# A hybrid encoder trunk on one core: the first attention queries moved ahead of the retention's second output projection, and the last two steps of a norm ranked as urgent

## The chip, the core and the metric

The kernel runs on one NeuronCore of a Trainium2 chip. The metric is the device time of one execution in microseconds (us); several runs are made and their median is compared. TensorE (PE) does the matmuls, VectorE (DVE) and ScalarE (ACT) the elementwise work, GpSimd (POOL) a few small operations and the accumulating DMAs, and SyncE (SP) issues all other DMAs.

## What is computed

Two layers of a hybrid mixer on a sequence of 512 tokens with 1024 channels, all in float32:

```python
def hybrid_layer(x, ...):
    h = rms_norm(x, norm_g)
    z = h @ w_in
    (c_glu, c_gate, r_q, r_k, r_v, r_gate, a_q, a_k, a_v, a_gate, g_logit) = jnp.split(z, offsets, axis=-1)
    y_conv = conv_module(c_glu, c_gate, conv_dw, conv_b, conv_ln_g, conv_ln_b) @ w_conv_out
    y_ret = retention_branch(r_q, r_k, r_v, r_gate, ret_decay, positions) @ w_ret_out
    y_attn = window_attention_branch(a_q, a_k, a_v, a_gate, q_norm_g, k_norm_g, attn_sink, positions) @ w_attn_out
    g = jax.nn.sigmoid(g_logit + b_gate).reshape(B, S, N_BRANCH, D)
    merged = g[:, :, 0] * y_conv + g[:, :, 1] * y_ret + g[:, :, 2] * y_attn
    return x + merged @ w_out
```

The convolution module is a gated depthwise convolution of 31 taps, a layer norm over the channels, SiLU and a gate. The retention has 4 heads (keys of 256, values of 512 channels) in both directions, a norm per head and a gate. The attention has 16 query heads of 64 channels and 4 key/value heads, a norm and a partial rotation of queries and keys, a window of 128 tokens to each side and a sink.

## The kernel before, in words

**Precision and tiles.** Every float32 operand of a matmul is kept as a rounded high part and a low part (the rest). One product of 128 rows is three matmuls: high by high, high by low, low by high (`mm3`). ScalarE makes the high part by a copy; VectorE makes the low part by a subtraction, or, for the weights named in `BY_DMA` (among them `or`, the retention's output projection), ScalarE writes the negated high part and a DMA that GpSimd issues adds the weight to it in SBUF. A weight tile `wraw` (128 x 1024) comes from DRAM on SP's queue into one of 4 buffers; `wh` and `wl` have 8 buffers each, of half a weight tile.

**Order.** The builder writes the program down as a list of operations, each with an engine, its dependences and a priority: the time on TensorE at which it was written down plus an offset, the urgency. `Plan.order` then plays the program through with a table of costs. On each engine it always takes, of the operations that are ready, the one with the smallest priority, and the order found so is the fixed program order of each engine; on the chip every engine takes its instructions in that order. Line 342, where the recorded instructions are issued, is therefore the line of all of them in the profile, and they are told apart by their tiles. PSUM has two pools of 4 banks, `pc` and `ps`.

**Layer.** `layer` runs four retention heads (`head`), then `attention`, then `finish`. Two tables place the rest of the work between them: `HEAD_FILL` names for each head h what is written down after its queries and values (h, 0), after its scores and values product (h, 1), after its transposes and gate products (h, 2), and, for odd h, between the columns of the output projection (h, "o"). There m counts the entries; for h = 3 they count from 1. The letters: C and T are input and taps of the convolution, R, S, L, K, P gate projections, V the keys and values of the attention (`kv`), W the transposes of the normed keys (`k_transposes`), and Q the projection of four query heads with their norm (`Q`). `ATT_FILL` does the same in attention; there X0 and X1 are the first two steps of `conv_stats`.

**The stretch around the first edit.** At the end of head 3 the program transposes the head's normed output (tile `on`, a `big` tile; 16 transposes with the identity in `cst`, 4 per bank of `ps`), VectorE multiplies each bank with its gate (`pp<-ps,pp`) and makes the low part (`big<-pp,big`), as it does for the other head, which is fetched from DRAM (`og`). These are the operands of the second output projection: 8 columns m = 0 to 7 of 24 matmuls each, weights `or`, in banks of `pc`. Before the change V0 stands at (3, 1) and its projection runs just ahead of the transposes; the norm of the keys (`qk_norm`: squares, sums `qk_v`, a power on GpSimd `qk_r`, products, all in a `ws` tile) is in VectorE's queue beside the gate products. W0 stands at (3, 2), and Q0 at (3, "o") with m = 1, so between columns 0 and 1. Q0 is 96 matmuls of 128x256 in two banks of `ps`, from two weight tiles.

**The stretch around the second edit.** `conv_stats` makes the layer norm's statistics of the convolution in four steps. Step 2 (after column 0 of the attention's output projection, `FIN_FILL`) sums the squares over the channels by four matmuls with `ones` (`pc<-ones,ws`), VectorE and GpSimd make the reciprocal root (`tr_v`, `tr_r`), and VectorE writes four diagonal blocks (`ws<-cst,tr_r`). Step 3 (after column 3) spreads them by one matmul (`pc<-ws,ones`), and ScalarE copies the result. `conv_finish` uses it.

Of the kernel before, what the change touches and what calls it, by code (L numbers as in the profile page):

```python
# [36 lines left out]
NORM_EARLY, EVAC_EARLY, SQUARES_LATE = -15000, -20000, 0  # L37
LOAD_EARLY, SPLIT_EARLY, TAPS_LATE, STATS_LATE = -20000, -16000, 150000, 15000
# [7 lines left out]

HEAD_FILL = {(0, 0): "P6 P7", (0, 1): "R0 R1 C0 T0", (0, 2): "C1 C2 R2 R3",
             (1, 0): "C3", (1, 1): "C4 C5 T1", (1, 2): "C6 R4", (1, "o"): "R5 C7 L0 L1 L2 S0 S1 S2", (2, 0): "T2 S3", (2, 1): "T3 R6", (2, 2): "T4 K0 K1 R7",
             (3, 0): "T5 K2", (3, 1): "T6 T7 K3 V0", (3, 2): "W0", (3, "o"): "Q0"}


C_A, C_B, C_GATE = 0, 1024, 2048
# [326 lines left out]
class Builder:  # L379
# [531 lines left out]
    def conv_stats(self, step):  # L911

        nc = self.nc
        y = lambda k: self.fetch("y", k, self.tile("yt", [P, S]), step == 0)
        with nc.urgency(STATS_LATE):
            if step == 0:
                cs = self.tile("ws", [P, 2, S])
                self.cs, self.rb = cs[:, 0, :], cs[:, 1, :]
                nc.vector.tensor_tensor(out=self.cs, in0=y(0), in1=y(1), op=ALU.add)
                for k in range(2, 8):  # L920
                    nc.vector.tensor_tensor(out=self.cs, in0=self.cs, in1=y(k), op=ALU.add)
            elif step == 1:
                pm = self.pc()
                self.mm(pm, self.ones, self.cs, True, True)
                for k in range(8):
                    yk = y(k)
                    nc.vector.scalar_tensor_tensor(out=yk, in0=pm, scalar=-1.0 / D, in1=yk, op0=ALU.mult, op1=ALU.add)
                    sq = self.rb if k == 0 else self.tile("pad", [P, S])
                    nc.scalar.activation(out=sq, in_=yk, func=AF.Square)
                    self.keep("yc", k, yk)  # L930
                    if k:
                        nc.vector.tensor_tensor(out=self.rb, in0=self.rb, in1=sq, op=ALU.add)
            elif step == 2:
                self.rstd_diag(self.rb, self.cs)
            else:
                nc.scalar.copy(out=self.rb, in_=self.spread(self.cs))
# [321 lines left out]
```

## Time and profile before

| what | value |
|---|---|
| median of 3 runs | 1960.28 us (1959.76 to 1960.9) |
| the profiled execution | 1959.06 us |
| its span, first to last instruction | 1957.3 us |
| mean granted TensorE clock | 0.998 |
| TensorE busy | 1931.5 us, 99% |
| VectorE busy | 1694.7 us, 87% |
| ScalarE busy | 1159.7 us, 59% |
| GpSimd busy | 230.3 us, 12% |
| moved by DMA | 348.98 MB, mean 178 GB/s |

A profile is one execution. Busy is the time in which an engine had an instruction running; matmuls are pipelined, so the time of one reaches into the next, and the distance between starts tells the pace. A wait is put down to the operation that ended last before the waiting instruction began. The granted clock is the share of TensorE's full speed that the chip allowed.

### The profile page before, as it was taken

Reading aid. Unit: us, or ns where it says so; the run is one execution under the profiler, and the core shown is the slowest. Engines: PE = TensorE matmul, PEld = TensorE weight load, DVE = VectorE, ACT = ScalarE, POOL = GpSimd, SP = SyncE. Lnnn points to the kernel's source line nnn. Section 1 sums busy time; section 2 is a strip of 40 time slices with the busy share of each in tenths; the row PEclk is TensorE's granted clock in tenths of the full one; section 3 lists DMA queues with packets and bytes.
Section 4 is the critical chain, followed back from the end, with each engine's and each line's share of the span. In section 5 each row is a group of like instructions: output and inputs, shape, how many; then the busy total and the mean of one; then the engine's idle time right before and its main releaser. Section 6 shows DMA issues by size and latency. Waiting matters only on the chain.

```text
span 1957.3 us, 32895 instructions
## 1 busy us (share of the span) xinstructions
PE 1931.5 (99%) x11812; PEld 1717.1 (88%) x11812; DVE 1694.7 (87%) x3122; ACT 1159.7 (59%) x2230; POOL 230.3 (12%) x284
## 2 busy tenths in 40 slices
PE   8999999999999999999999999999999989999999
PEld 6899999999987888878889999999899878887787
DVE  8989998899987898977688999989999788989772
ACT  5565566556555478854436555655565465789541
POOL 0001011110123010000000010111101240110000
PEclk9999999999999999999999999999999999999999
DMA  6377478765678623488523665787656785234772
GB/s 231 91 212 188 135 221 216 207 168 181 181 180 230 202 77 103 148 273 280 169 87 114 213 167 149 219 212 208 170 177 171 211 218 190 86 100 155 252 268 72
DMA packets 143875, 348.98 MB, mean 178 GB/s; under 512 B 16096, under 2 KB 16352, under 8 KB 143712
## 3 DMA queue, kind: packets, MB, share of 16 engines
q1 hardware_dynamic: 115776, 296.02, 45.2%
q0 software_dynamic: 27936, 50.87, 15.1%
q8 instruction: 92, 1.51, 0.3%
q14 instruction: 71, 0.58, 0.1%
HBM read 237.25 MB, written 58.72 MB: 151 GB/s over the span
## 4 chain that ended last, share of the span: by engine, by line
PE 91%; DVE 3%; issue 3%; DMA 2%; POOL 0%; ACT 0%; SPq 0%; POOLq 0%; DVEq 0%
PE pc L342 57%; PE ps L342 34%; DVE ws L342 1%; DMA wraw<-wpk 1%; DMA oa<-pp 1%; DVE yt L342 1%; POOL qk_r L342 0%; DVE wide L342 0%; DVE pp L342 0%; DMA pp<-cg 0%; DMA wl<-wraw 0%; DVE big L342 0%; DMA big<-xT 0%; DMA yt<-y 0%; DVE mid L342 0%
## 5 line engine op out<-in xcount | busy, mean ns | idle before, releaser
L342 PE MATMUL pc<-big,wh 128*128 128x256 f32 (+1 forms) x4848 | 1150.4, 327 | 9.9 <-DVE big L342 7.8
L342 PEld LDWEIGHTS pc<-big,wh 128*128 128x128 f32 x4848 | 809.2, 188 | 91.7 <-DVE big L342 11.0
L342 PE MATMUL pc<-big,wl 128*128 128x256 f32 (+1 forms) x2424 | 789.2, 327 | 0.0
L342 ACT CAST wh<-wraw 128x512 fp32r<-128x512 f32 x558 | 344.3, 621 | 399.6 <-PE pc L342 255.7
L342 PEld LDWEIGHTS pc<-big,wl 128*128 128x128 f32 x2424 | 455.1, 188 | 37.0 <-DVE wl L342 0.3
L342 DVE SCALAR_TENSOR_TENSOR yt<-pad,prm,yt 128x512 f32<-128x512 f32 x480 | 358.3, 746 | 4.4
L342 PE MATMUL ps<-wh,big 128*128 128x512 f32 (+1 forms) x1152 | 296.8, 346 | 6.8 <-ACT big L342 6.8
L342 DVE TENSOR_TENSOR wl<-wraw,wh 128x512 fp32r<-128x512 f32 x364 | 247.3, 685 | 33.9 <-ACT wh L342 31.1
L342 POOL DMA_DIRECT2D wl<-wraw x194 | 169.4, 900 | 851.1 <-ACT wl L342 498.8
L342 ACT CAST wh<-ws 128x512 fp32r<-128x512 f32 x264 | 162.1, 621 | 157.9 <-PE pc L342 81.2
L342 PEld LDWEIGHTS ps<-wh,big 128*128 128x128 f32 x1152 | 199.7, 189 | 36.2 <-ACT big L342 6.8
L342 PE MATMUL ps<-wl,big 128*128 128x512 f32 (+1 forms) x576 | 199.0, 346 | 0.0
L342 DVE TENSOR_TENSOR wl<-ws,wh 128x512 fp32r<-128x512 f32 x264 | 177.5, 685 | 5.4 <-ACT wh L342 4.5
L342 PE MATMUL ps<-big,wh 128*128 128x256 f32 x832 | 151.3, 279 | 0.0
L342 ACT ACTIVATE wl<-wraw 128x512 fp32r<-128x512 f32 x194 | 122.5, 632 | 15.5 <-PE ps L342 15.5
L342 PEld LDWEIGHTS ps<-big,wh 128*128 128x128 f32 x832 | 127.0, 188 | 0.2
L342 PEld LDWEIGHTS ps<-wl,big 128*128 128x128 f32 x576 | 108.8, 189 | 14.8 <-issue 0.2
L342 PE MATMUL ps<-big,wl 128*128 128x256 f32 x416 | 116.0, 279 | 0.0
L342 DVE TENSOR_TENSOR ws<-wraw 128x512 f32<-128x512 f32 x132 | 86.8, 684 | 15.0 <-DMA wraw<-wpk 14.9
L342 PE MATMUL ps<-big 128*128 128x512 f32 (+2 forms) x448 | 99.5, 345 | 0.1
L342 PEld LDWEIGHTS ps<-big 128*128 128x128 f32 x448 | 81.6, 188 | 16.9 <-DVE sm_m L342 1.0
L342 DVE TENSOR_TENSOR ws<-ws,wraw 128x512 f32<-128x512 f32 x132 | 90.2, 683 | 0.1
(124 smaller groups left out, 2092.5 us busy)
## 6 DMA issues: line engine op xcount, KB each, us to landing
wraw<-wpk SPq DMA_DIRECT2D x312, 512.0 KB, 4.1
wl<-wraw POOLq DMA_DIRECT2D x194, 256.0 KB, 5.2
g<-pp SPq DMA_DIRECT2D x48, 256.0 KB, 3.3
pp<-g SPq DMA_DIRECT2D x48, 256.0 KB, 4.3
rg<-pp SPq DMA_DIRECT2D x32, 256.0 KB, 2.7
pp<-rg SPq DMA_DIRECT2D x32, 256.0 KB, 4.6
yt<-y SPq DMA_DIRECT2D x32, 256.0 KB, 2.9
wide<-toe SPq DMA_DIRECT2D x16, 448.0 KB, 3.4
```

Of the source, the lines that this page charges most:

```text
L342: getattr(getattr(self.nc, op.engine), op.method)(**kw)
```

## The change

Two lines. In `HEAD_FILL`, Q0 moves from (3, "o") to (3, 2) and stands ahead of W0 there, so it is written down ahead of the key transposes and of all columns of the second output projection, and its two weight tiles come ahead of column 0's in the weights' order. In `conv_stats`, steps 2 and 3 get the urgency `EVAC_EARLY` (-20000) instead of `STATS_LATE` (+15000); steps 0 and 1 keep theirs.

```diff
@@ -46,7 +46,7 @@
 HEAD_FILL = {(0, 0): "P6 P7", (0, 1): "R0 R1 C0 T0", (0, 2): "C1 C2 R2 R3",
              (1, 0): "C3", (1, 1): "C4 C5 T1", (1, 2): "C6 R4", (1, "o"): "R5 C7 L0 L1 L2 S0 S1 S2", (2, 0): "T2 S3", (2, 1): "T3 R6", (2, 2): "T4 K0 K1 R7",
-             (3, 0): "T5 K2", (3, 1): "T6 T7 K3 V0", (3, 2): "W0", (3, "o"): "Q0"}
+             (3, 0): "T5 K2", (3, 1): "T6 T7 K3 V0", (3, 2): "Q0 W0"}
@@ -912,7 +912,7 @@
-        with nc.urgency(STATS_LATE):
+        with nc.urgency(STATS_LATE if step < 2 else EVAC_EARLY):
```

**First place: TensorE in layer 0, from the end of the keys' and values' projection (`ps<-wh,big` 128x512).** `ps<-cst,big` are the transposes of `on`, `pc<-big,wh` and `pc<-big,wl` the columns of the output projection, `ps<-wh,big` 128x256 is Q0, `ps<-cst,ws` are the key transposes. Before:

```order
L342 MATMUL ps<-wh,big 128x512
L342 MATMUL ps<-cst,big 128x128 x4
L342 MATMUL pc<-big,wh 128x512 x2
L342 MATMUL pc<-big,wl 128x512
L342 MATMUL ps<-cst,big 128x128 x12
L342 MATMUL pc<-big,wh 128x512 x2
L342 MATMUL pc<-big,wl 128x512
```

and with the change, first the start and then the end of Q0:

```order
L342 MATMUL ps<-wh,big 128x512
L342 MATMUL ps<-cst,big 128x128 x16
L342 MATMUL ps<-wh,big 128x256
L342 MATMUL ps<-wl,big 128x256
L342 MATMUL ps<-wh,big 128x256 x2
```

```order
L342 MATMUL ps<-wl,big 128x256
L342 MATMUL ps<-wh,big 128x256
L342 MATMUL pc<-big,wh 128x512
L342 MATMUL ps<-cst,ws 128x128 x8
L342 MATMUL pc<-big,wh 128x512
L342 MATMUL pc<-big,wl 128x512
```

All of Q0 now stands between the transposes of `on` and column 0, and the key transposes stand behind Q0 and one matmul of column 0; before, column 0 came first, then the key transposes, then Q0. In layer 1 one matmul of column 0 stays between the twelfth and the thirteenth transpose; the rest is the same.

**Second place: VectorE beside it in layer 0.** `big<-ps,big` are the low parts of the keys' and values' banks, `wl<-wraw,wh` weight splits (Q0's), `pp<-ps,pp` the gate products, `big<-pp,big` the low parts of the projection's operands, `qk_v` and `ws<-ws,qk_r` the norm of the keys. Before:

```order
L342 TENSOR_TENSOR big<-ps,big 128x4x64
L342 TENSOR_TENSOR big<-pp,big 128x512
L342 TENSOR_TENSOR big<-ps,big 128x4x64
L342 TENSOR_TENSOR wl<-wraw,wh 128x512 x2
L342 TENSOR_TENSOR pp<-ps,pp 128x512
L342 TENSOR_TENSOR big<-ps,big 128x4x64 x2
L342 TENSOR_REDUCE qk_v<-mid 128x8 x2
L342 TENSOR_TENSOR big<-pp,big 128x512
L342 TENSOR_SCALAR qk_v<-qk_v 128x16
L342 TENSOR_TENSOR big<-pp,big 128x512 x3
L342 TENSOR_TENSOR pp<-ps,pp 128x512 x3
L342 TENSOR_TENSOR ws<-ws,qk_r 128x1024
```

and with the change:

```order
L342 TENSOR_TENSOR big<-ps,big 128x4x64 x4
L342 TENSOR_TENSOR pp<-ps,pp 128x512
L342 TENSOR_REDUCE qk_v<-mid 128x8 x2
L342 TENSOR_TENSOR big<-pp,big 128x512
L342 TENSOR_SCALAR qk_v<-qk_v 128x16
L342 TENSOR_TENSOR big<-pp,big 128x512 x4
L342 TENSOR_TENSOR pp<-ps,pp 128x512 x2
L342 TENSOR_TENSOR ws<-ws,qk_r 128x1024
```

The two splits have moved ahead of these rows, the four low parts of the keys and values now come first, and one low part of the operands and one gate product have moved behind the step on `qk_v`.

**Third place: TensorE in layer 0, at the norm's last two steps.** The long rows are the columns of the attention's output projection. Before:

```order
L342 MATMUL pc<-ones,ws 128x1 x3
L342 MATMUL pc<-big,wl 128x512
L342 MATMUL pc<-big,wh 128x512 x2
L342 MATMUL pc<-big,wl 128x512
L342 MATMUL pc<-big,wh 128x512 x2
L342 MATMUL pc<-big,wl 128x512
L342 MATMUL pc<-ws,ones 128x512
```

and with the change, the steps one after the other:

```order
L342 MATMUL pc<-big,wh 128x512
L342 MATMUL pc<-ones,ws 128x1 x4
L342 MATMUL pc<-big,wh 128x512
```

```order
L342 MATMUL pc<-big,wh 128x512
L342 MATMUL pc<-ws,ones 128x512
L342 MATMUL pc<-big,wh 128x512
```

Before, one of the four matmuls with `ones` stood 48 rows ahead of the other three, and the spread 6 rows behind these. Now all four stand together, and the spread 48 rows behind them.

## Rows read from the trace of the kernel before

**Rows 1.** The page, busy us, share of the span and instructions of each engine.

```profile
PE 1931.5 (99%) x11812; PEld 1717.1 (88%) x11812; DVE 1694.7 (87%) x3122; ACT 1159.7 (59%) x2230; POOL 230.3 (12%) x284
```

**Rows 2.** TensorE's waits: line, waited for, us in total, times, longest us.

```profile
PE pc L342 <- DVE big L342: 7.8, 7, 2.6
...
PE pc L342 <- DVE ws L342: 3.1, 2, 1.6
```

**Rows 3.** TensorE's timeline, layer 0: start us, us, operation, count [idle before <-releaser].

```profile
596.75 0.60 PE L342 MATMUL ps<-cst,big 128*128 128x128 f32 x4
...
607.92 0.50 PE L342 MATMUL pc<-big,wh 128*128 128x512 f32 x1 [1.92 <-DVE big L342]
...
613.22 0.37 PE L342 MATMUL ps<-wh,big 128*128 128x256 f32 x1
...
624.20 0.39 PE L342 MATMUL pc<-big,wl 128*128 128x512 f32 x1
```

**Rows 4.** TensorE's timeline, the same stretch of layer 1.

```profile
1568.26 0.60 PE L342 MATMUL ps<-cst,big 128*128 128x128 f32 x4
...
1569.38 1.47 PE L342 MATMUL ps<-cst,big 128*128 128x128 f32 x12
...
1585.48 0.44 PE L342 MATMUL ps<-wh,big 128*128 128x256 f32 x1
```

**Rows 5.** VectorE's timeline, evacuations of two neighbouring columns of the projection, layer 0.

```profile
639.96 0.69 DVE L342 TENSOR_TENSOR pp<-pp,pc 128x512 f32<-128x512 f32 x1 [0.47 <-PE pc L342]
...
645.45 0.69 DVE L342 TENSOR_TENSOR pp<-pp,pc 128x512 f32<-128x512 f32 x1 [0.83 <-PE pc L342]
```

**Rows 6.** Windows: us, busy of PE, PEld, DVE, ACT, POOL, PEclk, DMA share, GB/s.

```profile
597.00:613.00 16.00, 11.94 (x50) 7.86 (x49) 14.45 (x28) 10.63 (x23) 7.17 (x4) 0.89 0.72 183
625.00:669.00 44.00, 44.00 (x202) 36.37 (x201) 38.83 (x67) 17.25 (x30) 10.70 (x12) 1.00 0.97 261
...
760.00:780.00 20.00, 20.00 (x142) 18.68 (x141) 15.68 (x40) 16.05 (x40) 0.38 (x2) 1.00 0.27 93
800.00:820.00 20.00, 19.89 (x99) 15.87 (x98) 19.21 (x46) 18.73 (x46) 0.47 (x2) 1.00 0.61 200
```

**Rows 7.** Timelines around the spreading matmul: TensorE and VectorE, layer 0; TensorE, layer 1.

```profile
867.88 0.40 PE L342 MATMUL pc<-big,wl 128*128 128x512 f32 x1
869.84 1.12 PE L342 MATMUL pc<-ws,ones 128*128 128x512 f32 x2 [1.56 <-DVE ws L342]
...
866.59 0.16 DVE L342 TENSOR_SCALAR tr_v<-pc 128x4 f32<-128x4 f32 x1 [0.55 <-PE pc L342]
...
868.92 0.87 DVE L342 TENSOR_SCALAR ws<-cst,tr_r 128x128 f32<-128x128 f32 x4
...
1842.33 1.12 PE L342 MATMUL pc<-ws,ones 128*128 128x512 f32 x2 [1.57 <-DVE ws L342]
```

**Rows 8.** VectorE's timeline beside the transposes and column 0, layer 0.

```profile
596.99 1.28 DVE L342 TENSOR_TENSOR wl<-wraw,wh 128x512 fp32r<-128x512 f32 x2
...
601.24 0.17 DVE L342 TENSOR_SCALAR qk_v<-qk_v 128x16 f32<-128x16 f32 x1
...
603.12 1.88 DVE L342 TENSOR_TENSOR pp<-ps,pp 128x512 f32<-128x512 f32 x3
606.03 1.23 DVE L342 TENSOR_TENSOR ws<-ws,qk_r 128x1024 f32<-128x1024 f32 x1 [1.03 <-POOL qk_r L342]
...
610.86 0.41 DVE L342 TENSOR_TENSOR ws<-mid 128x256 f32<-128x256 f32 x1
```

**Rows 9.** GpSimd's timeline, the power in the norm of the keys, layer 0.

```profile
601.49 4.51 POOL L342 TENSOR_TENSOR qk_r<-qk_v,mhalf 128x16 f32<-128x16 f32 x1 [12.63 <-DVE qk_v L342]
```

**Rows 10.** DMA issues from 600 to 665 us: operation, count, KB each, median us to landing.

```profile
wraw<-wpk SPq DMA_DIRECT2D x11, 512.0 KB, 5.3
wl<-wraw POOLq DMA_DIRECT2D x14, 256.0 KB, 5.6
...
md<-pp SPq DMA_DIRECT2D x8, 256.0 KB, 5.1
```

## The prediction, made before the changed kernel was run

> **What bounds the kernel now.** I read the page's busy shares first, then the list of who waits for whom, then TensorE's timeline in the two stretches that the change touches, and last VectorE's and the DMA there. The page says that TensorE is busy for 1931.5 of 1957.3 us [rows 1]. So nearly every microsecond that can be won is one in which TensorE stands still or runs slowly, and the list of waits says where these are [rows 2]: 7.8 us before matmuls of `pc` that wait for VectorE's `big` tiles, and 3.1 us in two places before matmuls that wait for VectorE's `ws`.
>
> The first sort sits where the second output projection of the retention begins. In layer 0 the transposes of `on` start at 596.75 us (call this T0) and the first matmul of Q0 (the queries, 128x256) starts at 613.22 [rows 3]. Between them stand 16 transposes, the 24 matmuls of column m = 0 and the 8 transposes of the normed keys. How long these take when nothing waits: 4 transposes end to end take 0.60 us and 12 take 1.47 [rows 3, 4], so 8 are 0.87 and 16 are 1.75; and a column takes 5.49 us, the distance between two evacuations of neighbouring columns (639.96 and 645.45) that both waited for TensorE [rows 5]. Together 8.11 us. The stretch took 613.22 - 596.75 = 16.47, so 8.36 us are lost, though the longest gap shown before a single matmul is 1.92 [rows 3]: each wait also empties the pipeline, and the granted clock was 0.89 in 597 to 613 us [rows 6], which is some 3.5 us at 1.2 instead of 2.4 GHz after matmuls that had come one by one, and costs half of that. Layer 1 shows the same from 1568.26 to 1585.48 [rows 4]: 17.22, so 9.11 lost. The cause is VectorE: it is busy for 14.45 of these 16 us [rows 6], with the low parts of column 0's operands, the gate products and the norm of the keys in one queue.
>
> The second sort is the spreading matmul of the convolution's norm (`pc<-ws,ones`). The matmul ahead of it starts at 867.88 and would let the next one start 0.23 later; the spread starts at 869.84 [rows 7]. That is 1.73 us, and layer 1 shows the same gap (1.57 against 1.56 [rows 7]). VectorE made the four diagonal blocks from 868.92 on, for 0.87 us [rows 7], behind a column's evacuation.
>
> **The change, part by part.** *Q0 ahead of the projection.* No matmul is added or removed. After the transposes TensorE now has Q0, 10.98 us of matmuls (613.22 to 624.20 [rows 3]) that need only weights and the old `hh`/`hl`, and column 0 comes behind it. VectorE's 14 us of work then lie beside Q0. What can still be late, per layer:
> - The transposes wait for the banks of the keys-and-values projection. Four of them and three filler matmuls of column 0 (0.44 + 0.69) filled the 1.12 us up to the next twelve in layer 1 [rows 4]. In layer 0 the fillers are gone, but the evacuations of the banks now stand first on VectorE and ScalarE. Between 0 and the fillers' 0.7; I take 0.5.
> - Q0's second bank is that of the second gate product. The last three products began at 603.12 [rows 8], so the second of all four ended about 7.0 after T0; the two weight splits (1.28 [rows 8]) no longer stand ahead of it, so 5.8. Q0 needs the bank after 1.75 + 0.5 + half of 10.98, at 7.7. Between 0 and 1; I take 0.2.
> - The key transposes now follow Q0's end, at about T0 + 13.3 (1.75 + 0.5 + 10.98). The normed keys were done at 610.86 + 0.41, T0 + 14.5 [rows 8]. Ahead of the scalar step at 601.24 that releases GpSimd's power, the two splits are gone in both layers, in layer 0 one low part of 0.6 too. The power takes 4.51 [rows 9], and what follows it from 606.03 to 611.27 is as long as before. So the keys are done 1.2 to 1.8 earlier, at 12.7 to 13.3. Bounds: 0, and 1.2 if they come no earlier than before; I take 0.5.
> - Column 0's last operand is written near the time of the keys and is wanted at its end, near T0 + 20, so that wait goes and none replaces it.
>
> This gives 8.36 + 9.11 - 2 x 1.2 = **15.1 us**. Of what the step carries along: its two weight loads (512 KB each) pass column 0's on SP's queue and are split by VectorE, so column 0's two accumulating loads are issued later on GpSimd's queue, but still ahead of the keys' power, 11 us before use. On GpSimd the second power (Q0's) now stands ahead of column 3's loads instead of column 5's. If it starts 4 us behind Q0's end (T0 + 13.3) and takes 4.51 again, they are issued near T0 + 22, land 5.6 later [rows 10], and are wanted at 13.3 + 0.87 + 3 x 5.49 = T0 + 30.6, so 3 us of cover are left; if that goes, TensorE waits what the landing takes beyond it.
>
> *The norm's last two steps as urgent.* The four matmuls with `ones` now stand together where the first of them stood, and the spread 48 rows of the order behind them, some 16 us. The diagonal is ready long before: 2 x 1.73 = 3.45 us go. In exchange 0.16 + 0.87 us of VectorE work [rows 7] stand ahead of the last operands of the attention's output projection; between 0 and 1 us per layer, I take 0.2. Net **3.0 us**. The finish of the convolution's branch starts earlier, which only adds cover.
>
> *The order inside attention* changes where the planner sees other ready times. Nothing is added. The longest single wait that the order leaves in these rows is 1.92 us [rows 3], so I bound it by -2 and +2 and take 0, since both ends are as near.
>
> Sum: 18.1 us. The profiled execution took 1959.06 us (span 1957.3 and 1.76 around it), 1.2 below the median of 1960.28. 1959.06 - 18.1 = 1941.0, and against the median 1942.2; I say 1942.
>
> **The rivals.** *Part of it comes back at once.* The key transposes stand in TensorE's queue ahead of column 0, and TensorE takes its matmuls in order: if the keys' norm is late (its power waits for squares that ScalarE does behind the evacuations) or column 3's weights are, all of it waits. For: margins of 0 to 3 us above. Against: the cover is worked out from rows. At 3 to 4 us per layer, 6 to 8 of the 18 are lost: 1948 to 1950.
>
> *VectorE takes it back in attention.* Its work is the same and has 7 us less per layer; it is busy for 19.21 of 20 us at 800 to 820 [rows 6]. If half of the time won is not absorbed, 7.5 us come back, 1950; if all of the first part, 1957. Against: it idles 4.3 of 20 us at 760 to 780 [rows 6], and its depthwise taps, which the planner ranks last, can slide towards that.
>
> *DMA becomes the bound, and the kernel slower.* A column moves 512 KB of weights, two accumulating loads of 256 KB and three tiles of 256 KB, 1.835 MB [rows 10]. While columns follow each other (625 to 669) the DMA engines are busy 0.97 of the time at 261 GB/s [rows 6]; at that pace a column would take 7.03 us, not 5.49. So far Q0 lay between columns 0 and 1 and let transfers run ahead; now eight columns follow each other. If none is covered, 16 columns x 1.54 = 24.6 us come in against 18.1: 1966.7. It decides from 6.6 us per column on (18.1 / 16 above 5.49). Against: seven columns ran at 5.49 with no gap, and much of that 0.97 is prefetch and stores that nobody waits for. The Trainium skill ("DMA: Bandwidth & Descriptors", Issuing engines are not separate DMA queues) says that transfers of SP and GpSimd share the same 16 engines, which speaks for this rival; its section Where 436 GB/s comes from puts a core's HBM limit near 358 GB/s, by which a column would need 5.1 us, the rival would fall away and the sum would stand. No stretch in the rows settles it: 261 GB/s is what was moved, not what could be.
>
> *The second part does nothing* (the matmuls with `ones` wait for the sum of squares instead): 3 us less, 1945, inside the range.
>
> **How the numbers follow.** Forecast, with the second part doing nothing inside it: 0.65, from 1938.5 (all 17.5 + 3.45 us, and a little of attention) to 1946. First rival 0.16, second 0.13 (0.03 of it within 0.2% of before), DMA 0.06 (0.02 of it with so much covered that nothing changes, 0.04 slower). Up to 1952 lie the first two and half of the second rival, 0.87, less what falls beside the forecast's bounds: 1938.5 to 1952. About 0.2%, 3.9 us, is what a measurement of this kernel can tell from no change: faster 0.91, same 0.05, slower 0.04.
>
> **What would show it.** In the new profile, the stretch from the transposes of `on` to the end of Q0 and column 0 takes 20 to 21 us instead of 27.5, with granted clock 1.00; the wait for `big` in the list falls from 7.8 to about 1; Q0's matmuls follow the transposes; the keys' transposes have at most 1 us ahead of them. The wait for `ws` before the spread is gone. The forecast is wrong if TensorE waits for `ws` or `ps` ahead of the key transposes for several us, if columns stand more than 5.6 us apart, or if gaps of more than 1 us appear in attention.

## The result and the profile after

The changed kernel took 1945.78 us (median of 4 runs, 1945.19 to 1946.74), the kernel before, on the same chip, 1960.59 (1959.76 to 1961.76). The ratio is 0.9924, with a 95% interval of 0.9909 to 0.9940: 14.8 us faster, where 18 were forecast. The profiled execution took 1945.19 us, with a span of 1943.4; before it was 1957.3, so the two traces account for 13.9 us.

The page of the changed kernel and its list of TensorE's waits, to be read against [rows 1, 2]:

```profile
PE 1927.2 (99%) x11812; PEld 1716.9 (88%) x11812; DVE 1692.2 (87%) x3122; ACT 1160.5 (60%) x2230; POOL 227.3 (12%) x284
```
```profile
PE ps L342 <- ACT big L342: 7.2, 1, 7.2
PE ps L342 <- DVE pp L342: 3.0, 5, 0.9
PE ps L342 <- DVE sm_m L342: 1.1, 3, 0.6
PE ps L342 <- ACT pp L342: 0.4, 2, 0.2
PE pc L342 <- DVE pp L342: 0.3, 1, 0.3
```

Both waits that the change aimed at are gone: 7.8 us for `big` and 3.1 for `ws`. The first line is the program's start, as it was before. What is new stands in lines two and three: 1.1 us for `sm_m`, and 3.0 for `pp`, where 1.8 were before.

TensorE's timeline of the changed kernel shows layer 0's stretch of [rows 3] and, from 1561.64 on, layer 1's of [rows 4]:

```profile
596.41 2.02 PE L342 MATMUL ps<-cst,big 128*128 128x128 f32 x16
598.37 0.39 PE L342 MATMUL ps<-wh,big 128*128 128x256 f32 x1
...
609.37 0.39 PE L342 MATMUL pc<-big,wh 128*128 128x512 f32 x1
609.60 1.03 PE L342 MATMUL ps<-cst,ws 128*128 128x128 f32 x8
...
1561.64 1.64 PE L342 MATMUL ps<-cst,big 128*128 128x128 f32 x12
1563.22 0.50 PE L342 MATMUL pc<-big,wh 128*128 128x512 f32 x1
1563.56 0.60 PE L342 MATMUL ps<-cst,big 128*128 128x128 f32 x4
```

In layer 0 the 16 transposes, Q0, the 8 transposes of the keys and column 0 follow each other without a gap. The windows (columns as in [rows 6]) give the granted clock:

```profile
597.00:617.00 20.00, 20.00 (x147) 18.48 (x146) 19.74 (x36) 17.71 (x34) 10.65 (x7) 1.00 0.83 215
617.00:663.00 46.00, 46.00 (x213) 38.25 (x212) 41.97 (x72) 18.53 (x34) 7.95 (x10) 1.00 0.87 252
```

The clock is 1.00 where it was 0.89. VectorE is fuller than it was, 19.74 of 20 us against 14.45 of 16, but TensorE no longer waits for it.

Where did the time go after that? Take one instruction that both traces have at each end of a stage and subtract its start times. VectorE's evacuations of columns serve (the first of [rows 5], and one of layer 1), and TensorE's transposes of the normed queries `ps<-cst,ws` near the end of attention. Of before:

```profile
1612.30 0.69 DVE L342 TENSOR_TENSOR pp<-pp,pc 128x512 f32<-128x512 f32 x1 [0.47 <-PE pc L342]
```
```profile
798.08 0.66 PE L342 MATMUL ps<-cst,ws 128*128 128x128 f32 x4 [0.69 <-DVE pp L342]
1770.01 0.66 PE L342 MATMUL ps<-cst,ws 128*128 128x128 f32 x4 [0.68 <-DVE pp L342]
```

The same instructions in the changed kernel (the first row, which the table doesn't use, is column 0's evacuation, the end of the stretch above):

```profile
615.95 0.69 DVE L342 TENSOR_TENSOR pp<-pp,pc 128x512 f32<-128x512 f32 x1
...
632.43 0.69 DVE L342 TENSOR_TENSOR pp<-pp,pc 128x512 f32<-128x512 f32 x1 [0.52 <-PE pc L342]
637.92 0.69 DVE L342 TENSOR_TENSOR pp<-pp,pc 128x512 f32<-128x512 f32 x1 [0.52 <-PE pc L342]
...
1598.16 0.69 DVE L342 TENSOR_TENSOR pp<-pp,pc 128x512 f32<-128x512 f32 x1
```
```profile
794.06 0.66 PE L342 MATMUL ps<-cst,ws 128*128 128x128 f32 x4 [0.91 <-DVE pp L342]
1759.14 0.66 PE L342 MATMUL ps<-cst,ws 128*128 128x128 f32 x4 [0.91 <-DVE pp L342]
```

| point | before | after | after minus before | the stage up to it |
|---|---|---|---|---|
| transposes of `on`, layer 0 | 596.75 | 596.41 | -0.34 | -0.3 |
| column's evacuation, layer 0 | 639.96 | 632.43 | -7.53 | **-7.2** |
| transposes in attention, layer 0 | 798.08 | 794.06 | -4.02 | **+3.5** |
| transposes of `on`, layer 1 | 1568.26 | 1561.64 | -6.62 | -2.6 |
| column's evacuation, layer 1 | 1612.30 | 1598.16 | -14.14 | **-7.5** |
| transposes in attention, layer 1 | 1770.01 | 1759.14 | -10.87 | **+3.3** |
| end of the span | 1957.3 | 1943.4 | -13.9 | -3.0 |

So the moved queries win 14.7 us, attention gives 6.8 back up to the point taken, and the stages behind it, which hold the norm's spread, win 5.6.

Not all of the 5.6 is the norm's. The matmul ahead of the spread and the third one behind it began at 867.88 [rows 7] and 871.26 us before, and at 858.08 and 859.63 now:

```profile
871.26 0.40 PE L342 MATMUL pc<-big,wl 128*128 128x512 f32 x1
```
```profile
858.08 0.40 PE L342 MATMUL pc<-big,wh 128*128 128x512 f32 x1
...
859.63 0.63 PE L342 MATMUL pc<-big,wh 128*128 128x512 f32 x2
```

That is 3.38 us against 1.55, so 1.83 per layer (layer 1 shows the same two times) and 3.7 in all. Most of the rest comes back in the last part of attention. A later point shows it, the same matmul of a column of its output projection, before and after:

```profile
858.50 0.62 PE L342 MATMUL pc<-big,wh 128*128 128x512 f32 x2
...
1831.46 0.39 PE L342 MATMUL pc<-big,wl 128*128 128x512 f32 x1
```
```profile
854.64 0.62 PE L342 MATMUL pc<-big,wh 128*128 128x512 f32 x2
...
1820.12 0.39 PE L342 MATMUL pc<-big,wl 128*128 128x512 f32 x1
```

From the column's evacuation in the table to this matmul, attention took 218.5 us in layer 0 and 219.2 in layer 1; now it takes 222.2 and 222.0. Of the difference 0.7 per layer is no loss: three of the four matmuls with `ones` stood behind this point before and stand ahead of it now. So 3.0 + 2.1 = 5.1 us are still lost at the end of attention, and the parts add up: 14.7 - 5.1 + 3.7, with 0.3 won ahead of the first stretch and 0.3 between the layers, make the 13.9.

In attention these are the longest of TensorE's new gaps in layer 0:

```profile
738.72 0.66 PE L342 MATMUL ps<-cst,wide 128*128 128x128 f32 x4 [0.60 <-DVE sm_m L342]
740.13 0.96 PE L342 MATMUL ps<-pp,big 128*128 128x512 f32 x3 [0.75 <-DVE pp L342]
```

Who keeps TensorE waiting is seen over the two blocks of scores before. A block is a group of four score operations of VectorE (`wide<-ps,cst,prm`); the windows run from the first of the sixth block to the first of the eighth, 719.6 to 744.1 us before and 712.0 to 742.4 after. Of each pair the first line is all work, the second the operations on `yt` alone, the convolution's taps (its columns are VectorE and ScalarE, clock, DMA share, GB/s). Before:

```profile
719.60:744.10 24.50, 24.50 (x171) 22.57 (x170) 22.62 (x51) 19.04 (x46) 3.24 (x3) 1.00 0.35 117
```
```profile
719.60:744.10 24.50, 5.21 (x7) 0.00 (x0) 1.00 0.35 117
```

After:

```profile
712.00:742.40 30.40, 28.70 (x185) 25.10 (x184) 30.08 (x64) 21.13 (x49) 3.29 (x3) 1.00 0.21 70
```
```profile
712.00:742.40 30.40, 11.94 (x16) 0.00 (x0) 1.00 0.21 70
```

Before the change VectorE had 22.62 us of work in this stretch, less than TensorE's 24.5. After it, 16 taps stand there instead of 7. VectorE has 30.08 us of work in 30.40, the stretch is 5.9 us longer, and TensorE can fill only part of that with matmuls from further behind. Counted by start times, 232 taps of layer 0 stood ahead of the third block before, and 223 do now: the nine have slid here from there, as TensorE now comes to the scores 7.5 us earlier.

### The profile page after: what moved, and what is told of

Its sections match the earlier page's. It is cut to its first block, busy times and chain, and to the rows that moved or that the text cites. A ratio compares the mean times of both kernels' runs of the same rounds, so it can differ in the third digit from the quotient of the medians.

```text
span 1943.4 us, 32881 instructions
## 1 busy us (share of the span) xinstructions
PE 1927.2 (99%) x11812; PEld 1716.9 (88%) x11812; DVE 1692.2 (87%) x3122; ACT 1160.5 (60%) x2230; POOL 227.3 (12%) x284
## 4 chain that ended last, share of the span: by engine, by line
PE 93%; DVE 3%; DMA 1%; ACT 1%; issue 1%; SPq 0%; POOLq 0%
PE pc L342 58%; PE ps L342 35%; DVE yt L342 1%; DMA wraw<-wpk 1%; DVE ws L342 1%; DVE wl L342 0%; DVE wide L342 0%; ACT wide L342 0%; DVE pp L342 0%; DVE big L342 0%; DMA wl<-wraw 0%; ACT pp L342 0%; DMA big<-xT 0%; ACT big L342 0%; DVE qk_v L342 0%
## 5 line engine op out<-in xcount | busy, mean ns | idle before, releaser
L342 PEld LDWEIGHTS ps<-wl,big 128*128 128x128 f32 x576 | 108.7, 189 | 14.8 <-DVE wl L342 0.3
```

Source lines behind the costliest of these rows:

```text
L342: getattr(getattr(self.nc, op.engine), op.method)(**kw)
```

## The experiments

**Which part won what**

`q0_only`: the moved queries alone (the diff is against the changed kernel, as everywhere below unless said).

```diff
-        with nc.urgency(STATS_LATE if step < 2 else EVAC_EARLY):
+        with nc.urgency(STATS_LATE):
```

> Only the queries are moved; the norm's four steps keep their old urgency. By TensorE's instructions of the two profiles the moved queries win 7.2 us in layer 0 and 7.4 in layer 1, attention gives 3.5 and 3.3 back, and the norm's spread wins 2.5 twice. Theory A (the loss in attention belongs to the moved queries: on VectorE's queue 14 of the last taps now stand at the seventh block of scores, 5 before): 14.6 - 6.8 = 7.8 won, 1952.8 us, with the waits for sm_m and pp at 738 to 743 us still there and the two waits for ws before the spread back. Theory B (the loss belongs to the norm's urgency): 14.6 won, 1946 us, and no wait of over 0.3 us at 738 to 743.

Measured: 1948.25 us, ratio 0.9948 (0.9935 to 0.9960), so 10.2 us faster than before (7.8 to 12.7). Of TensorE's waits the 3.1 us for `ws` are as in [rows 2], and in attention there is:

```profile
PE ps L342 <- DVE sm_m L342: 1.1, 3, 0.6
```

The wait for `sm_m` in attention is there without the norm's urgency, and the wait for `ws` is back: theory A in kind, with a gain between the two forecasts. To the end of attention this kernel gives 2.9 and 2.1 us back, not 3.5 and 3.3, and 14.7 - 5.0 = 9.7 is close to the 10.2.

`norm_only`: the norm's urgency alone, in the kernel before.

```diff
-        with nc.urgency(STATS_LATE):
+        with nc.urgency(STATS_LATE if step < 2 else EVAC_EARLY):
```

> Only the norm's last two steps are ordered as urgent; the queries stay behind the projection's first column. Theory A: the spread wins all of its 5.0 us, 1955.6 us, the waits for big before the projection stay at 7.8 us and attention has no new wait. Theory B (the loss in attention belongs to the norm's urgency): 5.0 - 6.8, so 1.8 us slower than before, 1962.4. The prediction's own term for this part was 3.0 us: 1957.6.

Measured: 1954.37 us, ratio 0.9980 (0.9971 to 0.9989), so 3.9 us faster (2.2 to 5.7). This holds the prediction's 3.0 as well as theory A's 5.0 and the 3.7 above, and excludes B. The two parts add up: 10.2 + 3.9 = 14.1, against 14.9 by the ratio of both together.

`w0_q0`: the keys' transposes (`W0`) ahead of the queries.

```diff
-             (3, 0): "T5 K2", (3, 1): "T6 T7 K3 V0", (3, 2): "Q0 W0"}
+             (3, 0): "T5 K2", (3, 1): "T6 T7 K3 V0", (3, 2): "W0 Q0"}
```

> The changed kernel, but the key transposes are recorded ahead of the queries instead of behind them; column 0 then fills the time ahead of the key transposes again, as before the change. On VectorE's queue 7 (layer 0) and 5 (layer 1) of the taps stand at the seventh block of scores, as before. Theory A (what won was that Q0 covers the wait for VectorE, and what lost was where the taps stand): the wait for big is back with about 7 us per layer, attention has no new wait, and what is left is the norm's 5.0: 1955.6 us. Rival (the gain came from anything else in the move, such as the later column 0 or its loads): within 3 us of 1945.8, with no wait before the projection.

Measured: 1948.87 us, ratio 0.9950 (0.9938 to 0.9963). TensorE's timeline and the window of layer 0:

```profile
598.74 0.50 PE L342 MATMUL pc<-big,wh 128*128 128x512 f32 x1 [0.44 <-ACT big L342]
600.03 0.50 PE L342 MATMUL pc<-big,wh 128*128 128x512 f32 x1 [0.79 <-DVE big L342]
```
```profile
596.00:612.00 16.00, 13.46 (x70) 10.57 (x69) 15.71 (x29) 12.17 (x25) 5.93 (x4) 0.89 0.79 199
```

With the keys' transposes first, column 0 is again ahead of Q0, the waits for its operands are back, and the clock is 0.89 again. By start times of the same instructions this stretch wins 1.5 us in layer 0 and 2.9 in layer 1 against before, not 7.2 and 7.5, and attention gives nothing back up to the transposes of the table (-0.4 and 0.0). Both halves of theory A are there in the trace. By the ratio the kernel wins 9.8 us against before, where the theory's sum is 5.0: the waits cost 5.7 and 4.6 us instead of the 7 per layer assumed. What makes the move worth its time is Q0 ahead of column 0.

**Is it the taps that VectorE is full of?**

`few_taps` and its control `few_taps_b` (the same line in the kernel before):

```diff
-            for k in range(TAPS):
+            for k in range(TAPS if c < 7 else 22):
```

> The changed kernel without the last 9 of the 31 taps of the last channel chunk (the sum of that chunk leaves these products out): 9 x 0.66 = 5.9 us less VectorE work per layer, all of it taken from the stretch between the sixth and the seventh block of scores, where 16 taps stand in the changed kernel and 7 before. Theory A (the 3.4 us per layer that attention gives back are VectorE's: taps that slid there): 6 to 7 us less than the changed kernel, 1939, with no wait of over 0.3 us where 738 to 743 us were. Rival (the waits there come from the order of scores and transposes, or from VectorE being full before): within 2 us of 1945.8.

> The control: the same 9 taps left out of the kernel before the change. Theory A (before the change VectorE hid these taps, since TensorE came 7 us later to the scores): within 2 us of before, 1959. Rival (taps cost time in either kernel): 5 us or more under before.

Measured: `few_taps` 1940.36 us, ratio 0.9908 (0.9895 to 0.9922), 5.4 us under the changed kernel by the medians and 3.1 by the ratios; `few_taps_b` 1955.71, ratio 0.9989 (0.9980 to 0.9998), about 2 us under before. The stretch from the sixth to the eighth block of `few_taps`:

```profile
712.50:737.00 24.50, 24.50 (x171) 22.58 (x170) 22.64 (x51) 19.05 (x46) 3.23 (x3) 1.00 0.35 117
```
```profile
712.50:737.00 24.50, 5.22 (x7) 0.00 (x0) 1.00 0.35 117
```

It is the stretch of before again, to the hundredth: 24.50 us, 7 taps. The waits for `sm_m` are gone from the list. The intervals of the two ratios just overlap, so the times alone would not settle it; the traces do. From the column's evacuation to the matmul of the attention's output projection, both layers together, leaving the taps out saves 6.6 us in the changed kernel and 2.6 in the kernel before. The 4.0 us between them are most of the 5.1 that attention loses, so theory A holds in the main: most of the loss is the nine taps that slid there. That it is VectorE's work in this stretch that counts, and not something particular to taps, `q_dma` below bears out.

**Can they stand elsewhere?**

`taps_100`, `taps_200` and `taps_20`: the planner's rank of the taps, here for the first:

```diff
-LOAD_EARLY, SPLIT_EARLY, TAPS_LATE, STATS_LATE = -20000, -16000, 150000, 15000
+LOAD_EARLY, SPLIT_EARLY, TAPS_LATE, STATS_LATE = -20000, -16000, 100000, 15000
```

> The changed kernel with one number changed: the planner ranks the depthwise taps 100000 behind instead of 150000, so that on VectorE's queue none of them stands behind the fourth block of scores (14 at the seventh block in the changed kernel). Theory A (VectorE idles 4.3 us at 670 to 680 us while taps are left for later, so the loss of 3.5 and 3.3 us in attention is a matter of order): 5 to 7 us less than the changed kernel, 1939 to 1941, and no wait of over 0.3 us at 730 to 745. Rival (VectorE is full there, whatever the order): 1945.8 within 1.5 us, with the waits in another place.

Measured: 1959.85 us, ratio 1.0007 (0.9998 to 1.0016): the whole gain is lost. Both forecasts were wrong. The window from the third to the fifth block of scores, all work and taps:

```profile
680.10:714.10 34.00, 30.20 (x117) 22.63 (x116) 33.07 (x69) 19.21 (x44) 3.66 (x3) 0.75 0.18 61
```
```profile
680.10:714.10 34.00, 17.15 (x24) 0.00 (x0) 0.75 0.18 61
```

24 taps now stand in these blocks, VectorE is full there (33.07 of 34.00), and TensorE, left waiting, is granted a clock of 0.75. By start times only two more than in the changed kernel stand between the second and the third block, where the idle time of 670 to 680 us was; the others were pulled in front of the next scores.

> The changed kernel with the taps ranked 200000 behind instead of 150000: 11 instead of 16 of them between the sixth and the eighth block of scores, 7 of them at the ninth and tenth, where VectorE idles 3 to 5 us per block. Theory A' (what costs is how many taps stand in the blocks where VectorE has no idle time; earlier ones cost more, as ranked 100000 behind they took 10 us per layer): 2 to 5 us less than the changed kernel, 1941 to 1944. Rival (VectorE's total is the bound and the place of the taps makes no difference): 1945.8 within 1.5.

Measured: 1945.24 us, ratio 0.9929 (0.9915 to 0.9943), no difference from the changed kernel (0.9924). From the sixth to the eighth block it has 10 taps and takes 28.3 us:

```profile
713.90:742.20 28.30, 28.30 (x188) 25.86 (x187) 27.26 (x61) 21.45 (x49) 4.13 (x3) 1.00 0.30 93
```

So the stretch itself became 2.1 us shorter, but at the matmul of the attention's output projection 1.0 us of it is left in layer 0 and 0.4 in layer 1. The rival's number came out; why the later blocks took it back was not separated.

> The changed kernel with the taps ranked 20000 behind: all 248 of a layer stand ahead of the first scores, 35 more than in the changed kernel, 23 us of VectorE work moved out of attention into a stretch (to 659 us) in which VectorE idles 12 us in its last 74. Theory A: no wait is left at 738 to 743, 7 us won there, and what does not fit into idle time ahead of attention costs up to 11 us per layer there: 1939 if the work of earlier stages has idle time for it, 1960 if not. Rival: 1945.8 within 1.5.

Measured: 1973.03 us, ratio 1.0075 (1.0063 to 1.0088). The largest of TensorE's waits in the first 300 us that the changed kernel does not have:

```profile
PE pc L342 <- DVE wl L342: 5.9, 2, 3.6
```

Ahead of attention the taps stand before the low parts of weights (`wl`). By start times TensorE loses 15 us against before between 155 and 175 us alone; there was no idle time for them. The miss was to look for idle time only in the last 74 us ahead of attention.

**Other work off VectorE, and a better version**

`q_dma`, `q2_dma` and `q12_dma`: the low parts of the queries' weights by accumulating loads, for all groups, for Q2, and for Q1 and Q2. The first:

```diff
-        dma = key[0] in BY_DMA and len(self.keys) % NSUB > 24
+        dma = key[0] in BY_DMA + ("q",) and len(self.keys) % NSUB > 24
```

> The changed kernel with the low parts of the queries' weights made by accumulating loads, as the retention's output projection has them, instead of by VectorE: per layer 16 operations of 0.68 us on VectorE become 16 copies of 0.6 us on ScalarE and 16 loads on GpSimd's queue (10.9 us of VectorE per layer, 5.4 of them for Q1 and Q2, ahead of or in the stretch where attention gives 3.4 back). Theory A (VectorE is full there: leaving 5.9 us of it out gave 5.4 us in all): 4 to 6 us less than the changed kernel, 1940 to 1942, no wait for sm_m or pp of over 0.3 us at 730 to 745. Rival (ScalarE, busy for 55.8 of 75 us there, or the loads' landing takes VectorE's place): 1945 or more, with waits for wl or for ScalarE.

> The same for Q2 alone, whose four low parts per layer (2.7 us) stand in the fullest stretch, between the sixth and the seventh block of scores. Theory A: 2.7 of the 3.4 us per layer can go, so 3 to 5 us less than the changed kernel, 1941 to 1943. Rival (as above): 1945 or more.

> The changed kernel with the low parts of Q1's and Q2's weights alone made by accumulating loads; Q0's are left to VectorE, since with Q0's moved too the transposes ahead of Q0 were split again and 2.2 us were lost there in layer 0 and 3.7 in layer 1 against the changed kernel. VectorE has 5.4 us per layer less between the scores' second and seventh block. Theory A (VectorE is full up to the seventh block, so each microsecond taken from it there counts until the 3.4 per layer are won): the stretch to Q0 as in the changed kernel and 5 to 6.8 us less in attention, 1939 to 1941. Rival (ScalarE's four copies more per group cost as much as VectorE wins, as where Q2 alone was moved and 2 to 3 us were won): 1942 to 1944.

Measured: `q_dma` 1941.97 us, ratio 0.9914 (0.9901 to 0.9928); `q2_dma` 1942.16, 0.9912 (0.9897 to 0.9927); `q12_dma` 1944.46, 0.9919 (0.9905 to 0.9933). Beside the changed kernel's 0.9924 they are 1.0 to 2.4 us better, which the intervals don't separate; by the medians `q_dma` and `q2_dma` are the fastest that compute everything, and lie in theory A's ranges, but by the ratios 2.0 and 2.4 us are less than the 4 and the 3 that it asks for at least. The stretch from the sixth to the eighth block in `q12_dma`, and its taps:

```profile
710.60:741.60 31.00, 29.98 (x191) 26.39 (x191) 30.59 (x65) 20.33 (x47) 3.54 (x3) 1.00 0.21 69
```
```profile
710.60:741.60 31.00, 11.90 (x16) 0.00 (x0) 1.00 0.21 69
```

The 16 taps are still there, as they are in `q2_dma`, and VectorE is busy for 30.59 of 31.00 us. In `q_dma` the same stretch has 10 taps:

```profile
712.00:735.50 23.50, 23.50 (x165) 21.92 (x165) 20.36 (x48) 19.16 (x45) 6.75 (x7) 1.00 0.44 101
```

It takes 23.5 us, and TensorE has no gap in it. From the column's evacuation to the matmul of the attention's output projection, both layers together, `q_dma` is 6.3 us shorter than the changed kernel, `q2_dma` 3.8 and `q12_dma` 2.5. So of the 5.4 us that `q2_dma` takes from VectorE in the two layers most came through in attention, of the 10.8 of `q12_dma` a quarter, with about 1 us left in its time, and `q_dma` wins back what attention had lost. For `q12_dma` the rival's number nearly came out, though the reason it gives, ScalarE, was not shown.

`q_dma` pays elsewhere. From the transposes of `on` to the column's evacuation it loses 2.3 us against the changed kernel in layer 0 and 0.2 in layer 1 (not the 3.7 that the expectation of `q12_dma` names), and 1.6 between the layers, for which no cause was separated. In layer 0 the transposes ahead of Q0 wait again, as its row of TensorE shows:

```profile
597.68 0.65 PE L342 MATMUL ps<-cst,big 128*128 128x128 f32 x4 [0.32 <-DVE pp L342]
```

`gp_taps`: the same nine taps on GpSimd.

```diff
+                elif c == 7 and k >= 22:
+                    z = self.tile("th", [P, S])
+                    nc.gpsimd.tensor_scalar(out=z, in0=pad[:, k:k + S], scalar1=w, scalar2=None, op0=ALU.mult)
+                    nc.gpsimd.tensor_tensor(out=y, in0=y, in1=z, op=ALU.add)
```

> The changed kernel with the last 9 taps of the last channel chunk made by GpSimd, as a product and a sum each, so that nothing is left out: VectorE has the same 5.9 us per layer less as where these taps were left out, and GpSimd 18 operations more, whose duration no row shows; it is busy for 8.5 of 75 us in that stretch. Theory A: 5 us less than the changed kernel, 1940 to 1942. Rival (GpSimd's operations take so long that the loads behind them on its queue or the norm's first step come late, or they slow VectorE's operations down): 1945 or more, with VectorE's 128x512 operations longer than 0.75 us beside them.

Measured: 1952.88 us, ratio 0.9967 (0.9954 to 0.9979), 7 us slower than the changed kernel by the medians. The rival's time held, and so did its first reason. GpSimd's groups, and then its and VectorE's timelines at one place:

```profile
L342 POOL TENSOR_SCALAR th<-pad,prm 128x512 f32<-128x512 f32 x18 | 31.3, 1751 | 2.1 <-DMA pad<-vd 2.1
...
L342 POOL TENSOR_TENSOR yt<-yt,th 128x512 f32<-128x512 f32 x18 | 23.6, 1311 | 11.4 <-DVE yt L342 11.1
```
```profile
737.91 2.94 POOL L342 TENSOR_TENSOR qk_r<-qk_v,mhalf 128x16 f32<-128x16 f32 x1
740.81 1.31 POOL L342 TENSOR_TENSOR yt<-yt,th 128x512 f32<-128x512 f32 x1
742.08 4.19 POOL L342 TENSOR_SCALAR th<-pad,prm 128x512 f32<-128x512 f32 x2
```
```profile
739.29 0.69 DVE L342 TENSOR_TENSOR wl<-wraw,wh 128x512 fp32r<-128x512 f32 x1
740.88 2.32 DVE L342 TENSOR_TENSOR ws<-ws,qk_r 128x1024 f32<-128x1024 f32 x1 [0.91 <-POOL qk_r L342]
```

A tap costs GpSimd 1.75 + 1.31 = 3.1 us, and VectorE 0.75. The power of the queries' norm (`qk_r`) stands behind taps on GpSimd's queue: its operand was ready at 733.6 us, it began at 737.91, and VectorE waits 0.91 us for it. GpSimd's products also slow some of VectorE's weight splits down (last section).

## Why the prediction held, and where it missed

The forecast of 1942 was 3.8 us low, inside its range. Its largest terms were right, and one taken as zero was not. That the time came out 0.2 us inside even the narrower range of the forecast without its rivals, 1938.5 to 1946, is luck in part: the second rival's mechanism was at work, and 1.3 us won elsewhere made up for some of it.

*The first stretch, 15.1 us.* Measured 7.2 + 7.5 = 14.7. Two slips nearly cancel. The 8.36 and 9.11 us called lost were too much, because the count of matmuls ahead of Q0 was wrong. The trace of before, in the window of that stretch for the tile `pc` alone, has 28, column 0's 24 and 4 of column 1:

```profile
596.70:613.20 16.50, 9.30 (x28) 5.30 (x28) 0.69 (x1) 0.00 (x0) 0.90 0.71 182
```

Four times 0.23 is 0.9 us per layer, so 7.4 and 8.2 were to be won. On the other side, of the 1.2 us of give-backs per layer only 0.2 came in layer 0, where the transposes, Q0's second bank and the keys' transposes waited for nothing, and 0.7 in layer 1: 0.3 ahead of Q0, where a matmul of column 0 still splits the transposes, and 0.4 in Q0 itself, which took 11.4 us there instead of 11.0, with no wait in it; the cause of these 0.4 is open. Column 3's loads stayed covered: its evacuation and the next one stand 637.92 - 632.43 = 5.49 us apart, as in [rows 5].

*The norm, 3.0 us.* `norm_only` gave 3.9 (2.2 to 5.7), so the term holds. By start times the spread won 1.83 us per layer, 3.7 in all, a little more than the 1.73 us wait, and of the 0.2 to be given back nothing shows there.

*The order inside attention, 0 with bounds of -2 and +2.* This is the step that failed: +3.5 and +3.3 up to the transposes of the queries, and 3.0 + 2.1 = 5.1 us by the end. The bound was taken from the longest single wait, but the loss is a sum over VectorE's backlog. The second rival named the mechanism ("VectorE takes it back in attention") and a price of 7.5 us, where 5.1 to 6.8 were measured. The argument against it failed: that the taps would slide towards the idle time of 760 to 780 us [rows 6]. They slid, but only as far as the sixth to the eighth block of scores, where VectorE had 1.9 us of 24.5 free before. With 5.1 us lost in attention instead of 0, 14.7 instead of 15.1 and 3.7 instead of 3.0 the sum is 13.3 us; the traces show 13.9.

*The other rivals.* Part of the first stretch at once: no wait ahead of the key transposes. DMA: while columns follow each other its share is 0.87 at 252 GB/s in layer 0, less than the 0.97 of [rows 6], but in layer 1 it is more:

```profile
1577.10:1620.00 42.90, 42.90 (x190) 35.15 (x189) 39.59 (x61) 19.02 (x34) 11.61 (x11) 1.00 1.01 281
```

Even there TensorE has no wait, and columns whose evacuation waited for TensorE stand 5.49 us apart. So a share near 1 did not bound the columns here, and nobody waited for that traffic, as the argument against said; what of it was prefetch and what stores was not separated. No run shows how much the DMA could have moved, so the Trainium skill's 358 GB/s ("DMA: Bandwidth & Descriptors", Where 436 GB/s comes from) is not tested by any run here.

*What was to show it.* The stretch to the end of Q0 and column 0 took 19.5 us (596.41 to VectorE's evacuation of column 0 at 615.95), half a microsecond under the forecast, with the clock at 1.00; the waits went as named. No single gap in attention is over 1 us, and still 5.1 are lost. That test looked at the wrong thing: many small gaps and fillers pulled forward don't show as one long gap.

## What to carry to other kernels

When TensorE is made to arrive earlier, look at what the next engine still has to do by then, stage by stage: busy time over the stretch with the work that will stand in it, not the longest wait and not the mean of the kernel. Low-priority filler work (here the taps) slides to wherever the planner finds a slot, and it costs nothing only where its engine has idle time left. Compare two traces by the start times of the same instruction at stage borders; that shows in one table what a list of waits hides. Take more than one point per stage: here 1.7 of the 6.8 us given back were won again a little further on.

## What was not expected of the hardware

VectorE and GpSimd can hold each other up. In the rows of `gp_taps` above, VectorE's 128x1024 product, which takes 1.23 us in [rows 8], took 2.32 beside a GpSimd sum that ended at 742.12: 1.24 us beside the sum and 1.08 behind it, to 743.20. GpSimd's next two products, with a mean of 1.75 us over all 18, took 4.19 together, 0.7 more. The Trainium skill ("SBUF — State Buffer", SBUF: two separate sides) describes such an exclusive lock, held for the whole instruction, between a VectorE operation with two inputs from SBUF and a GpSimd operation that reads SBUF; at this place the trace agrees, in both directions. At others it does not: the weight split at 739.29, with two inputs from SBUF, took its usual 0.69 us in the midst of GpSimd's power, and the 12 splits of that run that began during one of GpSimd's products took 0.73 us in the median and 1.11 at most, though the products ran on for 0.3 to 1.5 us after the splits began (GpSimd's spans are rough).

GpSimd's power in the keys' norm took 4.51 us before [rows 9] and 3.30 in the changed kernel, with the same operands; whether VectorE's operations beside it make the difference was not tried.

In `taps_100` the gaps cost a second time through the clock. The 0.75 of that stretch is a granted clock of 1.00 up to about 696.6 us and of 0.50 to 713.6, the higher and the lower of the two levels of 2.4 and 1.2 GHz. In the 6.5 us ahead of the fall TensorE had been idle for 1.7. In the changed kernel 2.0 us idle in the 6.0 from 737.5 on left the clock at 1.00; what makes the difference these runs don't show.
